# Grouped adaLN modulations and held Strassen quadrants in the down projections; square sums of key and query heads moved behind the next head's products

## The chip, the cores and the metric

One core of a Trainium2 chip runs the whole program. The metric is device time in microseconds of one execution, the median of several. Engines are named as in the profile: PE (matmul) and PEld (its weight loads), DVE, ACT, POOL, and SP, whose queue (SPq) issues nearly all DMAs of the part that is changed.

## The reference

One step of a two-layer encoder on 1152 tokens (1024 of a prompt, 8 x 16 of samples), model width 1024, feed-forward width 2816, all in float32. Layer 0 is RWKV-7 time mixing and a SwiGLU, layer 1 band attention and a SwiGLU. What matters here:

```
mod = silu(c) @ w_ada[l] + b_ada[l]            # 9 rows of c: one prompt, 8 samples; 6*1024 columns per layer
sh_m, sc_m, gt_m, sh_f, sc_f, gt_f = split(mod, 6)
shift, scale = split(silu(c) @ kv_ada_w + kv_ada_b, 2)
h = rmsnorm(x) * (1 + scale) + shift
k = rms_norm(per head of 64: h @ w_k);  v = h @ w_v;  q = rms_norm(per head: hq @ wb_q)
x = x + gt_f * ((silu(h @ w_gate) * (h @ w_up)) @ w_down)      # once in each layer
```

## The kernel before

Activations lie feature by feature: 128 features on the partitions, tokens along the row. Every large float32 product is made of three matmuls (`mm3`): both operands are split into a rounded part (`hi`, an ACT copy, L276) and a rest (`lo`, a DVE subtraction, L277), and hi*hi, hi*lo and lo*hi are summed in PSUM. Tokens are in two groups, `c` = 0 (512) and `c` = 1 (640). The Tile framework's scheduler orders each engine's instructions by a simulated timeline and sets the waits; each engine then runs its own row in order. A tile pool hands out a fixed number of buffers per tag; a new tile waits until a buffer of its tag is released.

The dense part (`dense`) runs after layer 0's time mixing: gate and up products (`gate_up`), the down projection (`down`) of layer 0, then `kv` (keys, values, the first two query heads), attention, and gate, up and down of layer 1.

`down` is one level of Strassen in Winograd's form: seven products `i` in the order 0, 1, 2, 4, 5, 6, 3, each a turn over four blocks `m` of 128 output features. A turn loads its operand from DRAM (`operand`, L1491: `h<-bd`, three pieces for each group, each with a raw, a hi and a lo tile of the tag `h0` or `h1`, 14 buffers each), and each `m` loads 11 weight blocks (`weights`, L1502: `rq<-in_wd` or `rq<-ws`) and issues 33 matmuls of 256 columns (c = 0) and 33 of 320 (c = 1). So both layers' down projections have 7*4*66 = 1848 matmuls. The four output quadrants are summed in `acc`, which `feats` allocates for the whole stage: four buffers of `h0` and four of `h1`. Finished quadrants are added to the residual `x` (`result`, L1529 to L1533; tile `xin` of the 11 buffers of the tag `e`), and in layer 0 their squares are summed (`sqa`).

In layer 0, `down` also computes the modulations of layer 1 and of the keys (`ada_steps`, units 12 to 27). A unit is 512 columns of the weight; four loads of 2 x 256 KB (`aw<-in_wada`, L264), after each of which four matmuls take 32 columns of `scT` (silu(c)) as weights and write the four 32-partition strips of one PSUM bank (`acc<-aw,scT`), the strip standing for a quarter of the contraction; an ACT copy of 512 columns (L226); and four matmuls with the constant `qs` (`acc<-cst,aw`), which sum the strips. `self.step(3)` advances this by three of 64 pieces per block `m`.

In `kv`, `head` computes 128 features of keys or queries of one group, in two parts for c = 1. Each part's `head_norm` copies the product out (ACT), squares it (ACT, L1648), sums the squares by a matmul with the block-ones constant (`acc<-ht,cst` or `O<-ht,cst`), takes the inverse root (`rsqrt2`) and multiplies. Meanwhile `end`, the generator `done`, computes the squares' sum of the next group over all features (`S<-sqa,cst`, `PT<-sqa,cst`) and then its normed features (`normed_split`, L1683 to L1689), which the products need.

Of the kernel before, what the change touches and what calls it, by code (L numbers as in the profile page):

```python
# [76 lines left out]
def prep(i):  # L77
    i = {k: np.asarray(v) for k, v in i.items()}
    d = {}
# [16 lines left out]
    d["wada"] = np.ascontiguousarray(wa.reshape(2, 4, 128, 28, 2, 256).transpose(3, 4, 0, 2, 1, 5)).reshape(28, 4, 128, 1024)  # L96
    par = {f"mix{m}": i["rw_mix"][0, m] for m in range(6)}
# [48 lines left out]
class Trunk:  # L146
# [54 lines left out]
    def ada_steps(self, units, tag="aux", bufs=1, tile=None, sbt=None):  # L201

        nc = self.nc

        def load(u, i):
            w = (tile or self.rawtile)()
            if not isinstance(w, tuple):
                w = w[:, :1024],
            n = 1024 // len(w)
            for j, t in enumerate(w):  # L210
                self.wload(t, self.a["wada"][u, i][:, j * n:(j + 1) * n])
            return [t[:, o:o + 256] for t in w for o in range(0, n, 256)]
        todo = [(u, i) for u in units for i in range(4)]
        ahead = None
        for u in units:
            ps = self.bank(tag, bufs)
            for i in range(4):
                w = ahead or load(*todo.pop(0))
                ahead = load(*todo.pop(0)) if todo and self.fetch_ahead else None
                c = slice(i // 2 * 256, i // 2 * 256 + 256)  # L220
                for q in range(4):
                    mm(nc, ps[32 * q:32 * q + 32, c], self.scT[:, i % 2 * 4 + q, :], w[q], i % 2 == 0, i % 2 == 1)
                if i < 3:
                    yield
# [8 lines left out]
            yield  # L233

# [1157 lines left out]
    def ffn(self, l, B, W, part1, xsrc, dst, done):  # L1392

        nc = self.nc
        spill = self.down_open(l)
        self.gate_up(spill(0), B, iter(W), (0,))
        for _ in part1:
            pass
        self.gate_up(spill(0), B, iter(W), (1,))
        for f in range(1, 22):  # L1400
            self.gate_up(spill(f), B, self.strassen_weights(l, f, nc.vector if f == 1 else None), (0, 1))
            for g in range(32 * (f - 1) // 21, 32 * f // 21):
                self.down_sums(l, g)
        return self.down(l, xsrc, dst, done)
# [61 lines left out]
    def down(self, l, xsrc, dst, done):  # L1466

        nc = self.nc
        gate = 48 * l + 40
# [4 lines left out]
        if l:  # L1474
            turns += [(i, (0, 1)) for i in (6, 3)]
            self.ada = iter(())
        else:
            turns += [(i, (c,)) for c in (1, 0) for i in (6, 3)]
            part512 = lambda: self.ev("aw")[:, 0:512]
            self.ada = self.ada_steps(range(12, 28), "acc", 1, lambda: (part512(), part512()), part512)  # L1480
# [15 lines left out]
        def weights(i, m):  # L1496
            src = {0: 0, 1: 1, 3: 3}.get(i)
            src = self.Ws[m][:, {5: 0, 2: 1, 6: 2, 4: 3}[i]] if src is None else self.a[f"wd{l}"][:, src, m * 1408:(m + 1) * 1408]
# [23 lines left out]
        def result(h, t, m, cs):  # L1522
            f = 4 * h + m
            x = self.ev("xin")[:, 0:576]
            for c in cs:
# [6 lines left out]
                if l == 0:  # L1532
                    squares(c, t, f, o)  # L1533
# [3 lines left out]

        for i, cs in turns:
# [4 lines left out]
            for m in range(4):  # L1543
                W = weights(i, m)
                d = self.wide()[:, 256:832]
                for c in cs:
                    for n, (j, k) in enumerate(ks):
                        s = slice(k * 128, (k + 1) * 128)
                        hi, lo = (X[c][j][h][:, k] for h in range(2))
                        self.mm3(d[:, part[c]], W[j][0][:, s], W[j][1][:, s], hi, lo, n == 0, n == 10)  # L1550
                for c in cs:
# [18 lines left out]
                self.step(3)  # L1570
                for _ in range(2):
                    next(end, None)
            if l == 0 and i == 3:
# [4 lines left out]
        return end  # L1578

    def dense(self, x2, x3, close):  # L1580
# [4 lines left out]
        with ExitStack() as ctx:  # L1585
            pool = lambda n, **k: ctx.enter_context(self.tc.tile_pool(name=n, bufs=1, reuse_waits="tile", **k))
            self.hps = {0: pool("h0")}
            with ExitStack() as c2:
# [13 lines left out]
                def done(c, x, st):  # L1602
                    if c == 1:
                        self.Ak = self.gain("kvn", 104)
                    X[c] = x, self.sq_done(st)
# [35 lines left out]
    def head_norm(self, pz, w, g, out, tag):  # L1641

        nc = self.nc
        nc.scalar.activation(out, pz, AF.Copy)
        aux = self.bank(tag, 1)[:, :w]
        ht = lambda: self.ev("ht", 5)[:, :w]
        v = ht()
        nc.scalar.activation(v, out, AF.Square)  # L1648
        mm(nc, aux, self.C("bo"), v, True, True)
# [4 lines left out]
    def head(self, n, c, W, H, g, dst):  # L1654

        for o, m in ((0, 320), (320, 320)) if c else ((0, 512),):
# [35 lines left out]
    def kv(self, H, X, end):  # L1692
# [5 lines left out]
        nw = 3  # L1698
        W = [self.halves(self.a["wk"][n]) for n in range(nw)]
# [7 lines left out]
        for n in range(nw, 8):  # L1707
            W = self.halves(self.a["wk"][n])
            for c in (1, 0):
# [3 lines left out]
        for n in range(4):  # L1713
            W = [h for u in range(2) for h in self.halves(self.a["wv"][n, u])]
            for c in range(2):
                for w in range((4, 5)[c]):
                    ws = slice(w * 128, (w + 1) * 128)
                    pz = self.wide()[:, 0:256]
                    for k in range(8):
                        ks = slice(k % 2 * 256, (k % 2 + 1) * 256)  # L1720
                        wh, wl = W[k // 2]
                        self.mm3(pz, H[c][0][k][:, ws], H[c][1][k][:, ws], wh[:, ks], wl[:, ks], k == 0, k == 7)
                    vt = self.ev("vt")[:, 0:256]
# [9 lines left out]
        for n in range(2):  # L1733
# [5 lines left out]
            if n == 0:  # L1739
                for e in range(2):  # L1740
                    self.qprep(0, e)
# [370 lines left out]
```

## Time and profile before

| | us |
|---|---|
| median of 3 runs (lowest, highest) | 3791.01 (3785.09, 3791.89) |
| the profiled execution | 3785.41 |
| its span, first to last instruction | 3783.6 |
| busy: PE, PEld, DVE, ACT, POOL | 3457.2, 3088.6, 2248.3, 1667.9, 769.7 |
| first product of down, layer 0 | 1807.26 |
| first key product | 2132.34 |
| first value product | 2275.43 |
| first product of down, layer 1 | 3518.13 |

The profiled execution's time lies 1.8 us above its span, and 5.6 us below the median of the three runs. The table's last four rows are starts in the timeline of PE. A stage that PE fills is read from the rows of PE: how long a run of matmuls takes and what stands between the runs. A timeline row merges like instructions: start, time from the first start to the last end, engine, line, operation, out<-in, shape, count, and in brackets the idle time ahead and who ended it. Float32 matmuls that are not split are recorded twice each (four matmuls of `aw` give x8).

### The profile page before, as it was taken

How to read it: one execution, taken by the hardware profiler on the slowest of the kernel's cores; microseconds unless marked ns; L12 is line 12 of the kernel's file. 1: busy time of each engine (PE TensorE's matmuls, PEld its weight loads, DVE VectorE, ACT ScalarE, POOL GpSimd, SP SyncE). 2: the span in 40 equal slices, each digit the busy share in tenths (PEclk: the TensorE clock that was granted, in tenths of full speed). 3: DMA queues.
4: the chain of work that ended last, by engine and by line, in shares of the span. 5: the costliest groups of instructions: out<-in, count | busy, mean ns of one | idle time of the engine just before them, and what ended most of it. 6: DMA issues, size and time to landing. Idle time of an engine off the chain costs nothing.

```text
span 3783.6 us, 74619 instructions
## 1 busy us (share of the span) xinstructions
PE 3457.2 (91%) x29078; PEld 3088.6 (82%) x29078; DVE 2248.3 (59%) x4380; ACT 1667.9 (44%) x3182; POOL 769.7 (20%) x743
## 2 busy tenths in 40 slices
PE   5788989999889799999999899789888899999999
PEld 3677768777667699999888879677667799999999
DVE  4666666765446765555446742666575776555555
ACT  4545546554223533333344452556564433333342
POOL 0000000000011066676100000000000156667100
PEclk9887899889689899999999999899999899999999
DMA  5776676677666434445788322445565334444764
GB/s 209 233 220 166 199 217 190 194 202 211 180 186 201 141 127 142 139 138 160 265 319 294 123 73 93 144 143 160 159 205 172 133 123 148 143 139 142 243 205 138
DMA packets 548579, 664.12 MB, mean 176 GB/s; under 512 B 137056, under 2 KB 409440, under 8 KB 543744
## 3 DMA queue, kind: packets, MB, share of 16 engines
q1 hardware_dynamic: 472912, 560.62, 46.7%
q0 software_dynamic: 22224, 80.36, 7.0%
q10 hardware_dynamic: 53088, 18.36, 2.1%
q8 instruction: 229, 3.75, 0.4%
q14 instruction: 126, 1.03, 0.1%
HBM read 482.63 MB, written 176.53 MB: 174 GB/s over the span
## 4 chain that ended last, share of the span: by engine, by line
PE 65%; DMA 13%; DVE 10%; issue 6%; ACT 4%; SPq 1%; POOL 1%; ACTq 0%; DVEq 0%; POOLq 0%
PE S L143 30%; PE PT L143 14%; PE acc L143 12%; PE st L143 3%; PE O L143 2%; DMA raw<-in_rw_o 1%; DVE h L277 1%; PE G L143 1%; PE PT L1937 1%; PE aux L143 1%; DMA TT<-Z 1%; DVE wlo L277 1%; DMA bt<-in_rel 1%; DMA xin<-x 1%; DMA h<-bd 1%
## 5 line engine op out<-in xcount | busy, mean ns | idle before, releaser
L143 PE MATMUL S<-h,w 128*128 128x256 f32 (+1 forms) x7374 | 1036.6, 299 | 23.9 <-ACT h L276 7.4
L143 PEld LDWEIGHTS S<-h,w 128*128 128x128 f32 x7374 | 1002.4, 191 | 46.2 <-issue 19.1
L276 ACT ACTIVATE w<-rq 128x512 fp32r<-128x512 f32 (+1 forms) x500 | 304.4, 614 | 661.4 <-PE S L143 290.0
L277 DVE TENSOR_TENSOR w<-rq,w 128x512 fp32r<-128x512 f32 (+1 forms) x500 | 384.4, 773 | 286.6 <-ACT w L276 247.9
L143 PE MATMUL PT<-h,w 128*128 128x256 f32 (+1 forms) x3714 | 532.0, 298 | 10.2 <-DVE h L277 3.8
L143 PE MATMUL acc<-mx,whi 128*128 128x384 f32 x1728 | 505.9, 370 | 37.2 <-ACT whi L276 15.4
L143 PEld LDWEIGHTS PT<-h,w 128*128 128x128 f32 x3714 | 506.4, 190 | 20.5 <-issue 7.8
L143 PEld LDWEIGHTS acc<-mx,whi 128*128 128x128 f32 x1728 | 335.5, 203 | 67.9 <-ACT whi L276 20.1
L143 PE MATMUL acc<-mx,wlo 128*128 128x384 f32 x864 | 314.9, 365 | 9.0 <-DVE wlo L277 9.0
L1373 POOL TENSOR_TENSOR t<-t,t 128x576 f32<-128x576 f32 (+1 forms) x132 | 221.9, 1682 | 262.9 <-ACT t L1380 154.0
L277 DVE TENSOR_TENSOR h<-h,h 128x1024 fp32r<-128x1024 f32 (+6 forms) x152 | 169.3, 1125 | 121.2 <-ACT h L276 111.2
L276 ACT ACTIVATE h<-h 128x1024 fp32r<-128x1024 f32 (+6 forms) x152 | 142.8, 950 | 147.8 <-DMA h<-bd 110.0
L143 PEld LDWEIGHTS acc<-mx,wlo 128*128 128x128 f32 x864 | 174.1, 202 | 21.6 <-DVE wlo L277 13.9
L277 DVE TENSOR_TENSOR wlo<-raw,whi 128x1024 fp32r<-128x1024 f32 x114 | 139.0, 1221 | 83.6 <-ACT whi L276 82.7
L276 ACT ACTIVATE whi<-raw 128x1024 fp32r<-128x1024 f32 x114 | 119.6, 1053 | 128.7 <-PE acc L143 61.6
L143 PE MATMUL S<-h,wh 128*128 128x320 f32 (+1 forms) x744 | 148.5, 348 | 12.7 <-DVE h L1685 4.7
L143 PE MATMUL acc<-h,wh 128*128 128x256 f32 (+1 forms) x864 | 137.9, 309 | 18.4 <-ACT wh L276 9.1
L1373 DVE TENSOR_TENSOR t<-S,t 128x576 f32<-128x576 f32 (+1 forms) x117 | 86.6, 740 | 113.9 <-PE S L143 113.9
L143 PEld LDWEIGHTS S<-h,wh 128*128 128x128 f32 x744 | 123.4, 195 | 31.3 <-ACT wh L276 6.3
L143 PEld LDWEIGHTS acc<-h,wh 128*128 128x128 f32 x864 | 121.2, 200 | 27.2 <-ACT wh L276 9.8
L1303 POOL TENSOR_TENSOR h<-h,h 128x256 f32<-128x256 f32 x12 | 11.0, 942 | 569.9 <-DMA vf<-in_wo 569.9
L1767 POOL MEMSET qbd<- 128x128 f32 x1 | 0.2, 204 | 560.8 <-PE S L143 560.8
(455 smaller groups left out, 5625.8 us busy)
## 6 DMA issues: line engine op xcount, KB each, us to landing
aw<-in_wada SPq DMA_DIRECT2D x128, 256.0 KB, 5.3
bd<-t SPq DMA_DIRECT2D x154, 160.0 KB, 1.9
rq<-in_wg SPq DMA_DIRECT2D x88, 256.0 KB, 2.9
rq<-in_wu SPq DMA_DIRECT2D x88, 256.0 KB, 2.6
ws<-in_wd SPq DMA_DIRECT2D x64, 352.0 KB, 3.6
ws<-ws SPq DMA_DIRECT2D x64, 352.0 KB, 3.3
bd<-t SPq DMA_DIRECT2D x152, 128.0 KB, 1.8
rq<-ws SPq DMA_DIRECT2D x72, 256.0 KB, 3.4
```

The costliest lines, as they stand in the source:

```text
L143: return nc.tensor.matmul(out, lhsT, rhs, start=start, stop=stop)
L276: self.nc.scalar.activation(hi, x, AF.Copy)
L277: self.nc.vector.tensor_tensor(lo, x, hi, ALU.subtract)
L1303: gp.tensor_tensor(out[j], x[j], y[j], op)
L1373: return eng.tensor_tensor(out, x, y, ALU.add)
L1767: nc.gpsimd.memset(self.qbd, 0.0)
L1937: nc.tensor.transpose(pt[:, j * 128:(j + 1) * 128], P[:, j * 128:(j + 1) * 128], self.C("ident"))
```

## The change

Modulations in layer 0's `down`: `ada_groups` replaces `ada_steps` for those 16 units. A unit is now 1024 columns, and a strip stands for 256 output columns instead of a quarter of the contraction, so a unit is 8 loads deep. Two depths are one step: 8 matmuls, the first of which holds the others behind it (`issue_after`), in 32 steps. The same 128 loads of 256 KB are made from a rearranged weight (`wadb`); of a step's two depths the first is loaded into two `e` buffers, the second into the two buffers of the tag `ws`, which the sums of down weights used before (`spare`). Eight copies of 256 columns and 8 x 2 closing matmuls (`acc<-aw,aw`, with the constant `qg`) take the place of 16 copies of 512 and 16 x 4 matmuls. A step is taken after every 44 matmuls of the projection.

On PE, the first modulations of layer 0's down projection; `S` is the PSUM tile of a block `m`, `h` operand pieces, `w` weights, and a row `x2` is two matmuls. Before:

```order
L143 MATMUL S_20087<-h_19934,w_20078 128x320
L143 MATMUL acc_20040<-aw_20041,scT 32x256 x2
L143 MATMUL S_20087<-h_19934,w_20077 128x320
L143 MATMUL S_20087<-h_19935,w_20077 128x320
L143 MATMUL S_20087<-h_19934,w_20078 128x320
L143 MATMUL acc_20040<-aw_20042,scT 32x256 x2
L143 MATMUL S_20087<-h_19934,w_20077 128x320
```

And now:

```order
L145 MATMUL S_20204<-h_19911,w_20188 128x256
L145 MATMUL acc_20027<-ws_20024,scT 32x256 x2
L145 MATMUL acc_20027<-ws_20023,scT 32x256 x2
L145 MATMUL acc_20027<-aw_20020,scT 32x256 x2
L145 MATMUL acc_20027<-aw_20019,scT 32x256 x2
L145 MATMUL S_20204<-h_19910,w_20189 128x256
```

The pairs that stood apart between the projection's matmuls now stand in one run of eight. Over the whole stage, PE's row had 54 runs of modulation matmuls (of 1, 2, 3, 4, 6 and 8 such rows: 29, 10, 1, 5, 8 and 1 times) and 16 runs of strip sums; it now has 35 (29 of four rows, 6 of two) and 8.

Down projection of layer 1: `down_last` replaces `down`. Its sums are three held tiles per group (`T[0]`, `T[2]`, `T[4]`), allocated with their turns, so that one to three `h0` and `h1` buffers are held where four were; finished quadrants go to a tile `o` of the tag `e`, both groups in one row, and are added to the residual in one instruction of 576 columns (or 448 and the samples' 128).

On SP's queue, right behind the last stores of layer 1's gate and up results (`bd<-t`). Before:

```order
L1418 DMA bd_1_3_2_32902<-t_38649 128x320
L1502 DMA rq_39108<-in_wd 128x512
L1502 DMA rq_39114<-in_wd 128x512
L1502 DMA rq_39120<-in_wd 128x384
L1529 DMA xin_39195<-x_110 128x256
...
L1502 DMA rq_39302<-in_wd 128x512
L1491 DMA h_39072<-bd_0_1_0_32873 128x1024
L1491 DMA h_39090<-bd_1_1_0_32894 128x1280
```

And now:

```order
L1475 DMA bd_1_3_2_32852<-t_38599 128x320
L1648 DMA h_39016<-bd_0_1_0_32823 128x1024
L1648 DMA h_39034<-bd_1_1_0_32844 128x1280
L1659 DMA rq_39052<-in_wd 128x512
L1659 DMA rq_39058<-in_wd 128x512
L1659 DMA rq_39064<-in_wd 128x384
L1648 DMA h_39022<-bd_0_1_1_32824 128x1024
```

The operand loads of turn 1 (`h<-bd`, second index 1) stood behind 30 rows, 22 loads of `xin` and eight of weights; they now start in the next row, and those of turn 2 start 13 rows after them.

Keys and queries: `head_norm` is cut in two at the square. The second half, from the square sum's matmul on, is emitted four of eight contraction steps into the next head's products (`head_end`). `kv` computes head 3 of group 1 first, so four heads of group 1 stand ahead of group 0's; head 3's weights are loaded and split once more for group 0. `done` yields once more before its square sum.

On PE, the end of key head 6 and the begin of head 7 (`S_24605` and then `S_24665` is head 6 of group 0, 512 columns; the next `S` and `PT` are head 7 of group 1). Before:

```order
L143 MATMUL S_24665<-h_23878,wh_24584 128x512
L143 MATMUL O_24653<-ht_24654,cst 128x320
L143 MATMUL acc_24692<-ht_24693,cst 128x512
L143 MATMUL S_24716<-h_23218,wh_24706 128x320
L143 MATMUL PT_24755<-h_23218,wh_24706 128x320
```

And now:

```order
L145 MATMUL S_24605<-h_23782,wh_24524 128x512
L145 MATMUL O_24618<-ht_24603,cst 128x320
L145 MATMUL acc_24669<-ht_24642,cst 128x512
L145 MATMUL S_24656<-h_23217,wh_24646 128x320
L145 MATMUL PT_24695<-h_23217,wh_24646 128x320
```

The scheduler has put the square sums where they stood. Among the first heads they do move: those of group 1 now stand 12 to 21 matmuls into the next part, and group 0's sum over all features (`PT<-sqa,cst`) stands behind two parts of products where it stood behind nearly four:

```order
L145 MATMUL S_23731<-h_23220,wh_23699 128x320
L145 MATMUL acc_23744<-ht_23729,cst 128x320
L145 MATMUL PT_23770<-sqa_20559,cst 128x512
L145 MATMUL S_23827<-h_23217,wh_23793 128x320
```

This last piece is of the changed kernel; `S_23731` is the second part of head 3.

The diff, cut to its core:

```diff
+    def ada_groups(self, spare):
...
+        ev = lambda: self.ev("aw")[:, 0:512]
+        steps = [(u, k) for u in range(8) for k in range(8)]
+        def load(n):
+            W = []
+            for (u, k), new in zip(steps[n:n + 2], (ev, spare)):
+                t = [new() for _ in range(2)]
+                for h in range(2):
+                    nc.sync.dma_start(t[h], self.a["wadb"][u, k][:, 512 * h:512 * h + 512])
+                W.append([x[:, o:o + 256] for x in t for o in (0, 256)])
+            return W
+        def close(u, sb):
+            ps = self.bank("acc", 1)
+            for j in range(2):
+                mm(nc, ps[:, j * 36:(j + 1) * 36], sb[:, j * 128:(j + 1) * 128], qg, True, True)
...
+        for n in range(0, 64, 2):
...
+            todo = [(k + j, q, W[j][q]) for j in (1, 0) for q in (3, 2, 1, 0)]
+            lead = product(*todo.pop(0))
+            with self.tc.issue_after(lead.ins):
+                for x in todo:
+                    product(*x)
...
+            if n < 62:
+                W = load(n + 2)
+            yield
...
-            part512 = lambda: self.ev("aw")[:, 0:512]
-            self.ada = self.ada_steps(range(12, 28), "acc", 1, lambda: (part512(), part512()), part512)
+        spare = lambda: self.wq.tile([128, 4, 176], F32, tag="ws", ..., bufs=2).rearrange("p a b -> p (a b)")[:, 0:512]
+        self.ada = self.ada_groups(spare)
...
+                        count += 3
+                        if count >= 44:
+                            count -= 44
+                            self.step()
...
-                self.step(3)
...
+    def down_last(self, gate, xsrc, dst):
...
+        def hold(n):
+            T[n] = [self.slot(c)[:, :4 * (256, 320)[c]].rearrange("p (m t) -> p m t", m=4) for c in range(2)]
...
+        for i in (0, 1, 2, 4, 5, 6, 3):
+            X = operand(i)
+            if i in (0, 2, 4):
+                hold(i)
...
     def head(self, n, c, W, H, g, dst):
...
-            x = self.halfraw()[:, :m]
-            self.head_norm(pz, m, g, x, self.one())
-            self.nc.sync.dma_start(dst[:, n, 512 * c + o:512 * c + o + m], x)
+                if k == 3:
+                    self.head_end()
+            self.ending = self.head_tail(pz, n, m, g, dst[:, n, 512 * c + o:512 * c + o + m])
+            next(self.ending)
...
     def kv(self, H, X, end):
         nw = 3
+        self.head(nw, 1, self.halves(self.a["wk"][nw]), H, kn[:, 0:1], self.kT)
+        for _ in range(3):
+            next(end, None)
         W = [self.halves(self.a["wk"][n]) for n in range(nw)]
...
-            for c in (1, 0):
+            for c in (1, 0)[n == nw:]:
                 self.head(n, c, W, H, kn[:, 0:1], self.kT)
...
-            if n == 0:
-                for e in range(2):
-                    self.qprep(0, e)
+                if n and not c:
+                    for e in range(2):
+                        self.qprep(0, e)
+        self.head_end()
```

More of the change, by code (lines that the diff above doesn't have):

```diff
@@ L233, in ada_steps, with product @@
             yield
+    def ada_groups(self, spare):
+        nc = self.nc
+        qg = self.ev("aw")[:, 0:36]
+        nc.sync.dma_start(qg, self.a["qg"])
+        ev = lambda: self.ev("aw")[:, 0:512]
[12 more added lines that the diff above has]
+                mm(nc, ps[:, j * 36:(j + 1) * 36], sb[:, j * 128:(j + 1) * 128], qg, True, True)
+            o = 48 + u * 8
+            bo = PAR["bada"] + o
+            view = lambda t: t.rearrange("p (g j) n -> p g j n", j=2)
+            bv = view(self.par[:, bo:bo + 8].rearrange("p (f o) -> p f o", o=1).broadcast_to([128, 8, 9]))
+            for j in range(2):
+                pv = ps[:, j * 36:(j + 1) * 36].rearrange("p (g n) -> p g n", n=9)
+                nc.vector.tensor_tensor(view(self.mod[:, o:o + 8, :])[:, :, j], pv, bv[:, :, j], ALU.add)
+        W, last = load(0), None
+        for n in range(0, 64, 2):
+            if last:
+                close(*last)
+                last = None
+            if steps[n][1] == 0:
+                ps = self.bank("acc", 1)
+            u, k = steps[n]
+            todo = [(k + j, q, W[j][q]) for j in (1, 0) for q in (3, 2, 1, 0)]
+            def product(at, q, w):
+                return mm(nc, ps[32 * q:32 * q + 32, 0:256], self.scT[:, at, :], w, at == 1, at == 6)
+            lead = product(*todo.pop(0))
+            with self.tc.issue_after(lead.ins):
+                for x in todo:
+                    product(*x)
+            if k == 6:
+                last = u, ev()[:, 0:256]
+                nc.scalar.activation(last[1], ps[:, 0:256], AF.Copy)
+            if n < 62:
+                W = load(n + 2)
+            yield
+        close(*last)
     def gain(self, name, sc):
@@ L1403, in ffn @@
                 self.down_sums(l, g)
-        return self.down(l, xsrc, dst, done)
+        if l:
+            return self.down_last(48 * l + 40, xsrc, dst)
+        return self.down(48 * l + 40, xsrc, dst, done)
     def down_open(self, l):
@@ L1464, in down_sums, with down @@
         nc.sync.dma_start(self.Ws[m][:, :, j * 176:(j + 1) * 176], q)
-    def down(self, l, xsrc, dst, done):
+    def down(self, gate, xsrc, dst, done):
         nc = self.nc
-        gate = 48 * l + 40
         ks = [(j, k) for j, n in enumerate((4, 4, 3)) for k in range(n)]
@@ L1473, in down @@
         turns = [(i, (0, 1)) for i in (0, 1, 2, 4, 5)]
[L1474 to L1478, printed above, removed]
-            part512 = lambda: self.ev("aw")[:, 0:512]
-            self.ada = self.ada_steps(range(12, 28), "acc", 1, lambda: (part512(), part512()), part512)
+        turns += [(i, (c,)) for c in (1, 0) for i in (6, 3)]
+        spare = lambda: self.wq.tile([128, 4, 176], F32, tag="ws", name=self.nm("ws"), bufs=2).rearrange("p a b -> p (a b)")[:, 0:512]
+        self.ada = self.ada_groups(spare)
         acc, end = {}, iter(())
@@ L1531, in result @@
                 nc.sync.dma_start(dst[:, f, at], o)
-                if l == 0:
-                    squares(c, t, f, o)
+                squares(c, t, f, o)
         def add(o, a, b):
             nc.vector.tensor_tensor(o, a, b, ALU.add)
+        count = 0
         for i, cs in turns:
@@ L1569, in down @@
                     result(*{1: (0, 0), 5: (0, 1), 6: (1, 1), 3: (1, 0)}[i], m, cs)
-                self.step(3)
                 for _ in range(2):
                     next(end, None)
-            if l == 0 and i == 3:
+            if i == 3:
                 for g in (self.ada, end):
@@ L1604, in done @@
                         self.Ak = self.gain("kvn", 104)
+                    yield
                     X[c] = x, self.sq_done(st)
@@ L1641, in head_norm, with head_norm_steps @@
     def head_norm(self, pz, w, g, out, tag):
+        for _ in self.head_norm_steps(pz, w, g, out, tag):
+            pass
+    def head_norm_steps(self, pz, w, g, out, tag):
         nc = self.nc
         nc.scalar.activation(out, pz, AF.Copy)
-        aux = self.bank(tag, 1)[:, :w]
         ht = lambda: self.ev("ht", 5)[:, :w]
@@ L1648, in head_norm @@
         nc.scalar.activation(v, out, AF.Square)
+        yield
+        aux = self.bank(tag, 1)[:, :w]
         mm(nc, aux, self.C("bo"), v, True, True)
@@ L1661, in head, with head_end, head_tail @@
                 self.mm3(pz, wh[:, s], wl[:, s], H[c][0][k][:, o:o + m], H[c][1][k][:, o:o + m], k == 0, k == 7)
-            x = self.halfraw()[:, :m]
-            self.head_norm(pz, m, g, x, self.one())
-            self.nc.sync.dma_start(dst[:, n, 512 * c + o:512 * c + o + m], x)
+                if k == 3:
+                    self.head_end()
+            self.ending = self.head_tail(pz, n, m, g, dst[:, n, 512 * c + o:512 * c + o + m])
+            next(self.ending)
+    ending = iter(())
+    def head_end(self):
+        for _ in self.ending:
+            pass
+    def head_tail(self, pz, n, m, g, dst):
+        x = self.halfraw()[:, :m]
+        yield from self.head_norm_steps(pz, m, g, x, self.one())
+        self.nc.sync.dma_start(dst, x)
     def head_steps(self, n, c, o, m, W, H, g, dst):
```

73 lines of the change are left out of this document (72 added, 1 removed).

## The prediction

> **What bounds the kernel now.** I read the page's busy line and chain first, then busy time by stage, then PE's timeline in the stages that the change touches, then who was waited for there.
>
> ```profile
> PE 3457.2 (91%) x29078; PEld 3088.6 (82%) x29078; DVE 2248.3 (59%) x4380; ACT 1667.9 (44%) x3182; POOL 769.7 (20%) x743
> PE 65%; DMA 13%; DVE 10%; issue 6%; ACT 4%; SPq 1%; POOL 1%; ACTq 0%; DVEq 0%; POOLq 0%
> ```
>
> PE fills 91% of the span and carries 65% of the chain. In its stages only two things give time back: matmuls taken off its row, and waits in it. By stage (window, length, busy time of PE, PEld, DVE, ACT, POOL, granted clock, DMA share, GB/s):
>
> ```profile
> 1890.00:1950.00 60.00, 58.83 (x489) 50.82 (x488) 27.19 (x43) 24.67 (x38) 0.00 (x0) 1.00 0.93 337
> 1920.00:1940.00 20.00, 20.00 (x163) 18.07 (x159) 6.90 (x11) 10.71 (x17) 0.00 (x0) 1.00 1.02 385
> 2132.30:2275.40 143.10, 126.21 (x628) 104.51 (x626) 73.25 (x143) 74.50 (x157) 0.00 (x0) 0.96 0.18 60
> 3558.00:3572.00 14.00, 13.22 (x84) 12.93 (x85) 8.96 (x9) 7.45 (x12) 0.00 (x0) 0.77 0.53 193
> 3600.00:3616.00 16.00, 12.70 (x80) 12.08 (x81) 7.98 (x10) 5.89 (x7) 0.00 (x0) 0.89 0.68 214
> 3616.00:3779.00 163.00, 162.88 (x1218) 162.62 (x1216) 88.94 (x160) 56.88 (x90) 0.00 (x0) 1.00 0.52 166
> ```
>
> Layer 0's down projection (first two rows) is PE-bound with the DMA engines near full. The keys (third) have 16.9 us without PE. Layer 1's down projection (last three) runs full only from 3616 on; before that PE waits, and its clock falls to 0.77 and 0.89.
>
> The yardstick is that full stretch, from the chain in order of time, and the ends of both projections from PE's timeline:
>
> ```profile
> 3629.40 8.79 PE PT L143 x66
> 3638.19 17.59 PE S L143 x132
> ...
> 1807.26 3.18 PE L143 MATMUL PT<-h,w 128*128 128x256 f32 x25
> 2132.34 2.07 PE L143 MATMUL S<-h,wh 128*128 128x320 f32 x13
> 3518.13 3.27 PE L143 MATMUL S<-h,w 128*128 128x256 f32 x26
> 3773.76 5.12 PE L143 MATMUL S<-h,w 128*128 128x256 f32 x34
> ```
>
> 198 matmuls take 26.38 us, 0.1332 each, so the 1848 of one projection need 246.2. Layer 0's takes 2132.34 - 1807.26 = 325.1: 78.9 too many. Layer 1's takes 3778.9 - 3518.1 = 260.8: 14.6 too many. These two surpluses are nearly all that the change can reach.
>
> **Modulations in layer 0.** What a run of them costs is the distance to the next matmul of the projection:
>
> ```profile
> 1825.48 0.62 PE L143 MATMUL acc<-aw,scT 128*32 128x256 f32 x4 [1.46 <-DMA aw<-in_wada]
> 1826.03 0.71 PE L143 MATMUL S<-h,w 128*128 128x320 f32 x3
> ...
> 1974.76 0.64 PE L143 MATMUL acc<-aw,scT 128*32 128x256 f32 x8
> 1975.33 3.74 PE L143 MATMUL S<-h,w 128*128 128x256 f32 x29
> 1978.91 0.96 PE L143 MATMUL acc<-cst,aw 128*128 128x16 f32 x8
> 1979.72 3.36 PE L143 MATMUL S<-h,w 128*128 128x256 f32 x22
> 1983.01 1.07 PE L143 MATMUL acc<-aw,scT 128*32 128x256 f32 x16
> 1984.01 2.46 PE L143 MATMUL S<-h,w 128*128 128x320 f32 x15
> ```
>
> Two matmuls cost 0.55 us, four 0.57, eight 1.00: four strips run together, and a torn run wastes half. With the order's counts, the old 54 runs cost about 41 us (29 x 0.55, 10 x 0.57, 5 x 1.00; the ten longer ones at 0.45 for each four, 14 in all), the 16 strip sums 16 x 0.81 = 13.0. PE's idle time in the stage is 7.5 us, and the sum of squares takes 1.8. Of the 78.9, 15 are left, which I put down to re-entering the projection: 15 / 70 runs = 0.21 each. The trace doesn't show that mechanism apart; its bounds are 0 and 0.21.
>
> New: 29 x 1.00 + 6 x 0.57 = 32.4. The closing matmuls, 36 columns wide, don't occur in the trace; each pair lies between 0.2 us (a quarter of a strip sum) and 0.81 (a whole one); I take half, 0.4, as two of four are issued: 8 x 0.4 = 3.2. Re-entry 43 x 0.21 = 9.0. Together 44.6 instead of 69: 24 us less on PE, and with the bounds 18 to 25. The copies on ACT (eight of 256 columns for sixteen of 512) and the constant's small load lie beside PE, which is the fuller engine.
>
> What the change adds is a wait. The loads for a step's second depth have two buffers, so they can only be asked for when PE has read the last pair.
>
> ```profile
> L264 SPq DMA_DIRECT2D aw<-in_wada x128: 327/383/1521, 1822.7 to 2071.9; - x128
> DMA to landing us min/median/max: 2.6/5.3/7.9
> ```
>
> The pair is free half-way through a step's run and needed at the next one: 44 x 0.1332 + 0.21 + 0.5 = 6.6 us later. Two issues (0.38 each) and the median landing make 6.1, the quickest 3.4, the slowest 8.7. So at the median nothing waits, at the worst 2.1 us in each of 32 steps, 67 us. Were landings spread evenly over 2.6 to 7.9, the mean wait would be 0.4 us, 13 in all; the long landings before belong to bursts of six or seven loads, and pairs go out mostly alone now, so I take 0.25, 8 us. What waits behind it: every later projection matmul, as PE runs in order, and on SP's queue the weight loads behind the pair's. The first load's wait (1.46) may stay. Net for the stage: -24 + 8 = -16.
>
> The DMA engines carry the same bytes in less time: 337 GB/s at a share of 0.93 would become about 355 (337 x 325 / 309) at 0.98. The Trainium skill (DMA: Bandwidth & Descriptors, Where 436 GB/s comes from) puts the HBM limit for one core at about 358 GB/s, which would leave no room in this stretch of the stage; by it, gains beyond 6% there would be lost, 2 us at most. The row at 1920 moved 385 GB/s, so on this core the limit lies higher, and the sum stays.
>
> **Held quadrants in layer 1.** PE waits for the operands of turns 1 and 2:
>
> ```profile
> 3558.10 0.58 PE L143 MATMUL S<-h,w 128*128 128x256 f32 x1 [3.45 <-ACT h L276]
> 3559.36 2.72 PE L143 MATMUL S<-h,w 128*128 128x256 f32 x11 [0.68 <-DVE h L277]
> ...
> 3607.68 0.39 PE L143 MATMUL PT<-h,w 128*128 128x256 f32 x1 [2.28 <-ACT h L276]
> ...
> 3550.70 0.90 SPq L1491 DMA_DIRECT2D h<-bd  x2
> ```
>
> The load behind the first wait goes out at 3550.70, since the quadrants hold four of 14 buffers and a turn needs nine, and because it stands behind the `xin` loads. With one buffer held, all of turn 1's raw tiles fit beside turn 0's, and the order issues them right behind the stores, some 15 us earlier; the landing was about 6. So waits of 3.45 + 0.68 + 2.28 and some 1.3 of smaller ones go, 7.7 us, and the slow clock that follows them: 14 x 0.23 + 16 x 0.11 = 5.0. That is 12.7 of the 14.6; 0.94 at the start stays. I take -12, between 0 (operands are late for another reason) and -13.7. What could be late next are weights (`rq<-in_wd`), which share SP's queue with the earlier operand loads; at a DMA share of 0.6 there is room.
>
> The Trainium skill (TensorE: Matmul & The Clock Gate, What's actually happening) has the clock halved after an idle window of about 3.4 us, until as long a busy one has passed. By it only the first wait brings a slow spell, about 1.7 us lost, and the gain would be 9 to 10. The trace agrees with the fall after the 3.45 wait (0.77 over 14 us), but shows 0.89 around the 2.28 one as well, so I keep 12.
>
> At the end:
>
> ```profile
> 3778.92 0.82 DVE L1536 TENSOR_TENSOR h<-S,h 128x256 f32<-128x256 f32 x2 [7.12 <-PE S L143]
> 3779.66 0.94 DVE L1174 SCALAR_TENSOR_TENSOR h<-h,mod,xin 128x256 f32<-128x256 f32 x2
> ```
>
> Two additions, then one residual of 576 columns (about 0.8) where the first store went out after one of 256 (0.5): +0.3.
>
> **Keys and queries.** PE's waits from 2132 to 2276:
>
> ```profile
> PE S L143 <- DVE h L1685: 4.7, 2, 3.0
> PE acc L143 <- ACT ht L1648: 4.2, 5, 1.1
> PE O L143 <- ACT ht L1648: 3.6, 3, 1.3
> PE PT L143 <- DVE kk L337: 2.6, 1, 2.6
> ...
> 2143.10 12.77 PE L143 MATMUL S<-h,wh 128*128 128x320 f32 x67 [1.65 <-DVE h L1685]
> 2153.28 0.43 DVE L1520 TENSOR_TENSOR sqa<-sqa,kk 128x256 f32<-128x256 f32 x1 [0.53 <-ACT kk L1519]
> 2156.25 1.02 PE L143 MATMUL PT<-sqa,cst 128*128 128x512 f32 x2
> ```
>
> Square sums waited 4.2 + 3.6 = 7.8. The order leaves those of the later heads where they were, with their waits of about 1.2; among the first heads some three waits of a microsecond go, and most of the 2.6 behind `PT`. Against that, `PT<-sqa,cst` now stands two parts earlier: PE gets there about 7 us before 2156.25, at 2149 to 2150, and the last square is there at 2153.7: a new wait of some 4 us. The extra split of head 3's weights (1.4 us on DVE) may delay the 4.7. Bounds: -8 (all square sums) and +5 (the new wait and nothing gained); I take -1. Value blocks and the two query heads keep their order: 0.
>
> **Sum.** -16 - 12 + 0.3 - 1 = -28.7 on the profiled 3785.41 gives 3756.7; on the median of the runs, 5.6 higher, 3762. I predict 3759.
>
> **Rivals.**
> 1. Just-in-time pairs make it slower. Without them the change gains 24 + 12 + 1 = 37, so it turns at 37 / 32 = 1.16 us per step; the slowest landing gives 2.1, 67 us: 3785 + 30 = 3815. For it: the DMA share of 0.93. Against: the median leaves 0.5 us of slack, and a waiting PE also thins the traffic. Chance 0.05.
> 2. The pairs and the crowded DMA engines take two thirds of layer 0's gain: -24 + 18, in all -19: 3766 to 3772. Chance 0.20.
> 3. Layer 1's operands come earlier, but PE waits for weights instead: -4 in place of -12, in all -21: 3764 to 3770. Chance 0.10.
> 4. Pairs never wait, and the keys' waits go too: -24 - 13 - 7 = -44: 3741 to 3747. Chance 0.15.
> 5. Several terms fail together and nothing beyond 0.2% is left: 3780 to 3790. Chance 0.05.
>
> The forecast has 0.45, with 3750 to 3765 as its own range. 3738 to 3776 takes in rivals 2, 3 and 4 and leaves 1 and 5, and the outer ends of the bounds, outside. Faster by over 0.2% (7.6 us, about what can be told from no change) holds for the forecast and rivals 2 to 4: 0.90; 0.05 each for the rest.
>
> **What will show it.** Layer 0's projection should last about 309 us (325 before), with runs of x16 a microsecond long and the waits for `ws<-in_wadb` summing below 10 us; over 25 means rival 2, over 37 rival 1. Layer 1's should last about 249, at a clock of 1.00 throughout, with no wait for `h` above 1 us. The keys should show one wait of 3 to 5 us at `PT<-sqa,cst` and end-of-head waits as before. If layer 0's runs of eight cost more than 1.1 us, strips don't run together in the new order, and the first term falls.

## The result, and the profile after

The changed kernel takes 3775.6 us (median of 10 runs, 3764.3 to 3788.8) where the kernel before takes 3792.6 in the same series: a ratio of 0.9949, 95% interval 0.9934 to 0.9965. By that ratio it is 19 us (13 to 25) faster; the medians are 17 us apart. A second series (e12 below) gave 0.9947 (0.9925 to 0.9968). One run of e1, one of e3 and one of the kernel before took 11% to 86% longer than the others of their kernel, and the ratios leave them out. The prediction had 3759, with 3750 to 3765 as the forecast's own range and 3738 to 3776 as the outer one. The sign is right, and the gain is about 60% of what was forecast: 3775.6 lies outside the forecast's own range and 0.4 us inside the end of the outer one. The profiled execution, 3766.4 us with a span of 3764.6, is among the quicker ones.

The stages, from PE's timeline of the changed kernel (start, length, engine, line, operation, shape, count): the first row of layer 0's down projection, of the keys, of layer 1's down projection, and the last.

```profile
1801.87 3.15 PE L145 MATMUL PT<-h,w 128*128 128x256 f32 x25
...
2129.42 3.31 PE L145 MATMUL S<-h,wh 128*128 128x320 f32 x20
...
3512.22 3.27 PE L145 MATMUL S<-h,w 128*128 128x256 f32 x26
...
3750.38 8.95 PE L145 MATMUL S<-h,w 128*128 128x256 f32 x66
```

Layer 1's projection ends at 3759.3 and lasts 247.1 us (260.8 before). Layer 0's lasts 327.5, which is longer than the 325.1 before, although its matmul work shrank. The waits of PE in that stage tell where the gain went (who waited for whom: total, times, longest), first of the kernel before:

```profile
PE S L143 <- DVE sqa L1520: 3.5, 1, 3.5
PE acc L143 <- DMA aw<-in_wada: 1.6, 2, 1.5
```

and of the changed kernel:

```profile
PE S L145 <- DVE sqa L1572: 10.9, 1, 10.9
PE acc L145 <- DMA ws<-in_wadb: 5.2, 2, 3.7
PE PT L145 <- DVE h L1587: 3.2, 2, 2.2
PE S L145 <- ACT h L331: 3.2, 3, 1.7
PE S L145 <- DVE h L332: 2.0, 3, 0.8
```

With the smaller ones PE waits 26 us where it waited 7.3. The runs of modulations themselves came out as costed:

```profile
1965.40 0.64 PE L145 MATMUL acc<-ws,scT 128*32 128x256 f32 x8
1965.85 0.61 PE L145 MATMUL acc<-aw,scT 128*32 128x256 f32 x8
1966.40 4.41 PE L145 MATMUL S<-h,w 128*128 128x320 f32 x32
...
1981.22 0.53 PE L145 MATMUL acc<-aw,aw 128*128 128x36 f32 x4
1981.58 4.46 PE L145 MATMUL PT<-h,w 128*128 128x256 f32 x32
```

Eight matmuls (two rows of x8) take 1.00 us, a closing pair 0.36. And each of the two long waits is followed by a slow clock (window, length, busy PE, PEld, DVE, ACT, POOL, granted clock, DMA share, GB/s):

```profile
1824.60:1827.00 2.40, 2.35 (x18) 1.08 (x19) 0.00 (x0) 0.00 (x0) 0.00 (x0) 0.50 1.01 382
1827.00:1837.00 10.00, 10.00 (x64) 10.00 (x64) 1.95 (x3) 1.79 (x3) 0.00 (x0) 0.81 0.61 210
...
2102.50:2107.00 4.50, 4.47 (x15) 3.69 (x16) 0.91 (x2) 2.23 (x4) 0.00 (x0) 0.50 0.35 110
```

That is 0.5 x 2.4 + 0.19 x 10 = 3.1 us lost behind the first and 0.5 x 4.5 = 2.2 behind the second.

The wait of 10.9 us has a history, which the chain of work in order of time shows. In the kernel before, a loop through DVE, SP's queue and the DMA engines was already on the chain at that place:

```profile
2084.17 0.21 DVE h L1179
2084.38 0.02 issue
2084.40 0.32 SPq L1531
2084.72 0.05 issue
2084.76 0.02 SPq L1529
2084.78 0.03 issue
2084.81 4.39 DMA xin<-x
```

DVE finishes a residual, SP issues its store (`x<-h`), right behind it the load of the next `xin`, and DVE waits for that landing. In the changed kernel the same loop runs straight into PE's square sum (`S<-sqa,cst`, here the head of the last row):

```profile
2090.25 4.02 DMA xin<-x
2094.30 0.56 DVE h L1229
2095.29 2.29 DMA xin<-x
2097.61 0.56 DVE h L1229
2098.56 2.31 DMA xin<-x
2100.89 0.56 DVE h L1229
2101.48 0.48 ACT kk L1571
2101.98 0.50 DVE sqa L1572
2102.53 13.04 PE S L145 x83
```

One turn of the loop costs 3.3 us with a landing of 2.3, and 5 to 9 us between 2067 and 2086, where DVE starts these residuals at 2066.9, 2075.8, 2080.7 and 2085.8. PE finished group 1's last product at about 2076.6 (before: 2093.0); the square sum could start at 2102.5 (before: 2105.0). In PE's timeline, first of the kernel before:

```profile
2104.96 2.50 PE L143 MATMUL S<-sqa,cst 128*128 128x320 f32 x4 [3.48 <-DVE sqa L1520]
...
2102.53 2.50 PE L145 MATMUL S<-sqa,cst 128*128 128x320 f32 x4 [10.92 <-DVE sqa L1572]
```

Of the 16 us that PE came earlier by the clock of the trace (5.4 of them from ahead of this stage), the loop passed on 2.5. Counted from the stage's first product, the square sum starts 300.7 us in, where it started 297.7 us in: the work that PE was spared did not bring the end of the loop forward.

### The profile page after: what moved, and what is told of

Its sections match the earlier page's. It is cut to its first block, busy times and chain, and to the rows that moved or that the text cites. A ratio compares the mean times of both kernels' runs of the same rounds, so it can differ in the third digit from the quotient of the medians.

```text
span 3764.6 us, 74365 instructions
## 1 busy us (share of the span) xinstructions
PE 3433.4 (91%) x28982; PEld 3079.2 (82%) x28982; DVE 2244.8 (60%) x4366; ACT 1660.5 (44%) x3176; POOL 769.9 (20%) x743
## 4 chain that ended last, share of the span: by engine, by line
PE 65%; DMA 13%; DVE 10%; issue 6%; ACT 4%; SPq 1%; POOL 1%; ACTq 0%; DVEq 0%; POOLq 0%
PE S L145 30%; PE PT L145 14%; PE acc L145 12%; PE st L145 3%; PE O L145 2%; PE PT L2098 1%; DMA raw<-in_rw_o 1%; DVE h L332 1%; PE aux L145 1%; PE G L145 1%; DMA TT<-Z 1%; PE Y L145 1%; DMA h<-bd 1%; DVE wlo L332 1%; DMA Z<-T 1%
## 5 line engine op out<-in xcount | busy, mean ns | idle before, releaser
L145 PE MATMUL PT<-h,w 128*128 128x256 f32 (+1 forms) x3714 | 527.2, 297 | 10.3 <-DVE rq L1428 3.8
```

Source lines behind the costliest of these rows:

```text
L145: return nc.tensor.matmul(out, lhsT, rhs, start=start, stop=stop)
```

## The experiments

Totals scatter by up to 25 us among runs of one kernel, so the stages were compared as well, each read from PE's timeline of one profiled execution. The columns are lengths in us: layer 0's down projection; keys; values to the end of layer 1's gate and up products; layer 1's down projection; and all of them. The last column is the ratio to the kernel before, by the timed runs.

| kernel | down 0 | keys | between | down 1 | sum | ratio (95%) |
|---|---|---|---|---|---|---|
| before | 325.1 | 143.1 | 1242.7 | 260.8 | 1971.6 | |
| changed | 327.5 | 138.0 | 1244.8 | 247.1 | 1957.5 | 0.9949 (0.9934 to 0.9965) |
| e12, changed again | 326.1 | 140.0 | 1242.3 | 246.4 | 1954.8 | 0.9947 (0.9925 to 0.9968) |
| e1, modulations only | 326.2 | 139.2 | 1239.7 | 258.3 | 1963.3 | 0.9963 (0.9951 to 0.9975) |
| e2, held quadrants only | 326.4 | 144.4 | 1246.9 | 247.2 | 1964.8 | 0.9975 (0.9958 to 0.9992) |
| e3, keys and queries only | 332.9 | 136.8 | 1242.0 | 257.2 | 1968.8 | 0.9969 (0.9955 to 0.9984) |
| e4, stores on POOL's queue | 321.2 | 134.3 | 1248.9 | 246.5 | 1950.9 | 0.9924 (0.9898 to 0.9949) |
| e6, xin asked for early | 322.6 | 139.2 | 1241.6 | 246.4 | 1949.8 | 0.9938 (0.9914 to 0.9962) |
| e8, pairs in e | 327.4 | 137.5 | 1241.0 | 247.1 | 1952.9 | 0.9932 (0.9911 to 0.9952) |
| e11, xin in ws | 307.5 | 136.3 | 1240.6 | 247.4 | 1931.8 | 0.9906 (0.9874 to 0.9937) |
| e5, xin in ws and early | 308.4 | 136.4 | 1237.4 | 246.9 | 1929.1 | 0.9889 (0.9868 to 0.9909) |
| e7, e5 and POOL's queue | 307.8 | 136.7 | 1247.3 | 247.5 | 1939.3 | 0.9898 (0.9878 to 0.9918) |
| e9, before with xin in ws, early | 325.8 | 134.6 | 1245.2 | 259.5 | 1965.1 | 0.9976 (0.9959 to 0.9994) |
| e10, e5 with the old heads | 310.6 | 136.9 | 1241.0 | 247.3 | 1935.8 | 0.9900 (0.9876 to 0.9924) |

**The parts alone.** e1 is the kernel before with `ada_groups` in place of `ada_steps`:

```diff
-            self.ada = self.ada_steps(range(12, 28), "acc", 1, lambda: (part512(), part512()), part512)
+            self.ada = self.ada_groups(spare)
```

> The kernel before with only the grouped modulations in layer 0's down projection. The changed kernel's trace has that stage at 1801.87 to 2129.42, 327.5 us against 325.1, although its runs of eight cost 1.00 us as forecast. Theory A (the end of the stage is held by the chain of residual loads, residuals and stores behind the sum of squares, which has not moved): PE saves 10 to 16 us and waits that much longer for sqa, so the wait ahead of S<-sqa,cst is 12 to 18 us (3.5 before), the stage lasts 322 to 328 and the kernel takes between -4 and +3 us against before. Rival B (the two-buffer pairs are what eats the gain): the waits for ws<-in_wadb sum to over 10 us and the wait for sqa stays below 6. Rival C (the fourth head and the added yield spoil layer 0's end, not the groups): with neither of them here the stage is 305 to 312 long and the kernel 12 us or more faster.

```profile
PE S L145 <- DVE sqa L1575: 9.5, 1, 9.5
PE acc L145 <- DMA ws<-in_wadb: 3.9, 2, 2.9
```

The stage (326.2) and the place of the wait are theory A's; rival C falls, and so does B: the pairs' waits stay small. The wait is shorter than A's 12 to 18, but others beside it grew: 23 us in all in this stage, against 7.3. The kernel is faster by 14 us (10 to 19), more than A had. Of the profiled execution's stages, the first two account for 2.8 of these, the others for 5.5, and the rest shows in none (see the last section). The three parts alone (e1, e2, e3) were timed at 14, 9.5 and 12 us, 35 together, where the whole change is worth 19; by the sums of the stages they are worth 8.3, 6.8 and 2.8, 18 together, where the whole is worth 14.

e2 has `down_last` for layer 1 alone:

```diff
+        if l:
+            return self.down_last(48 * l + 40, xsrc, dst)
         return self.down(l, xsrc, dst, done)
```

> The kernel before with only the held quadrants of layer 1's down projection. In the changed kernel's trace that stage lasts 247.1 us (3512.22 to 3759.33) against 260.8. If this part works alone: 247 to 249 us with no wait for h over 1 us, the clock at 1.00, and the kernel 12 to 14 us faster, which is two thirds of the whole change (19 us). If it needs the other parts: under 8 us.

The stage lasts 247.2: the whole gain of 13.6 us is there without the other parts. The timed ratio gives 9.5 us, less than the 12 to 14 expected, with an interval (3 to 16) that holds them.

e3 has the heads cut in two, the fourth head ahead and the extra `yield`:

```diff
                 def done(c, x, st):
...
+                    yield
                     X[c] = x, self.sq_done(st)
...
+        self.head(nw, 1, self.halves(self.a["wk"][nw]), H, kn[:, 0:1], self.kT)
+        for _ in range(3):
+            next(end, None)
```

> The kernel before with only the change of keys, queries and the extra yield ahead of the sum of squares. In the changed kernel's trace the keys last 138.0 us against 143.1, and from the values to layer 1's down projection 1244.8 against 1242.7. If the parts add up: keys 137 to 140, the kernel 2 to 6 us faster. If the 5 us of the keys come only from arriving late (operands already there, since PE had waited 10.9 us for sqa just before): keys 141 to 144 and the kernel within 2 us of before.

The keys get 6.3 us shorter and the stage ahead of them 7.8 longer: together 469.7 against 468.2, so nothing is gained up to the first value product. In the longer stage PE waits 10.3 us (7.3 before), 2.3 of them at an addition of DVE just ahead of the keys, and the granted clock is 0.93 in the first 50 us and 0.84 in the last 33 (1.00 and 0.94 in the first 50 and the last 25 before). Neither expectation foresaw that; the timed ratio (12 us faster, 6 to 17) is not explained by any stage that the edit touches.

**The chain of residual loads.** e4 takes the stores off SP's queue:

```diff
-                nc.sync.dma_start(dst[:, f, at], o)
+                nc.gpsimd.dma_start(dst[:, f, at], o)
```

> The changed kernel with the stores of layer 0's finished quadrants (x<-h) on POOL's queue instead of SP's, so that no load of xin stands behind a store that waits for a residual. Theory A1 (SP's order makes the chain load, residual, store, load, of 3.3 us for each result): the residuals of group 1 come up to a landing earlier each, the wait for sqa falls from 10.9 to below 4 us, the kernel is 6 to 10 us faster than the changed one. Rival A2 (the xin load waits for the buffer that the last residual frees, whatever stands ahead on SP): the residuals stay 3.3 us apart, the wait stays at 9 to 12, same time within 2 us. Rival A3 (the DMA engines, near full up to 2060, deliver late): the landings of xin stay at 4 to 6 us up to there, and the wait falls by 3 us at most.

```profile
2108.84 2.50 PE L145 MATMUL S<-sqa,cst 128*128 128x320 f32 x4 [5.06 <-DVE sqa L1572]
```

The wait halves and the stage is 6 us shorter: between A1 and A3. DVE still waited for a landing at most residuals, and the last six of group 1 started 3.1, 3.3, 3.8, 1.5 and 3.0 us apart, nearly the spacing that A2 had. So the store's place in SP's queue was only a part of the loop.

e6 asks for `xin` at the beginning of its block of products, from the same buffers `e`; e8 leaves `xin` alone and loads both depths of a modulation step into `e`:

```diff
+                xs = fetch(*RES[i], m, cs) if i in RES else None      # e6, behind weights(i, m)
...
-        spare = lambda: self.wq.tile([128, 4, 176], F32, tag="ws", ...
+        spare = lambda: self.ev("aw")[:, 0:512]                       # e8
```

> The changed kernel with the loads of xin asked for at the beginning of their block, still from the buffers e: a control for the run with xin in its own two buffers. In the order the loads still stand right behind the stores of the last result. Theory A1 (what counts is that a load stands behind the store of the residual before it): as the changed kernel, wait for sqa 9 to 12 us, time within 3 us. Rival (asking early is enough): wait below 5, 6 us or more faster.

> The changed kernel with both depths of a modulation step loaded into the buffers e, none into the two of the tag ws; nothing else changed. If the just-in-time pairs cost what the prediction took (0.25 us for each of 32 steps): waits of the modulations fall from 5.4 us to under 2, and the stage gets 3 to 5 us shorter at most, less what then waits for sqa. If they cost nothing beyond the first load's wait: the stage lasts 325 to 330 as now, with the time taken from the modulations added to the wait for sqa. If the buffers e were short: waits for xin grow and the kernel is 3 us or more slower.

e6 brings 5 us in the stage and leaves a wait of 8.3: mostly A1, a little of the rival. e8 settles the pairs. Without them the modulations wait no less:

```profile
PE acc L145 <- DMA aw<-in_wadb: 9.9, 6, 4.3
PE PT L145 <- DVE h L1587: 6.8, 2, 4.6
```

The modulations wait 9.9 us instead of 5.4, and the stage stays at 327.4, as its second expectation had it, but that one had the wait for `sqa` grow, and here none is left. The second row is the same chain in another place: DVE runs its row in order, so an addition that frees a PSUM bank stands behind a residual that waits for `xin`, and PE waits for the bank ahead of the square sum (the residual starts at 2103.64, the addition at 2104.58, PE at 2105.14).

e11 differs from e8 by one line (beside the definition of `two`), which gives `xin` the two `ws` buffers; e5 has the early request as well:

```diff
         def result(h, t, m, cs):
             f = 4 * h + m
-            x = self.ev("xin")[:, 0:576]
+            x = two()          # two buffers of the tag ws
```

> The changed kernel with the two ws buffers given to xin instead of the modulations (which take all four tiles of a step from the buffers e), and each load of xin asked for at the beginning of its block of products, so that a load can stand one result ahead. With stores moved to POOL's queue the residuals came closer but the wait for sqa was still 5.1 us. Theory A (the chain of residual loads holds the end of layer 0's stage): with loads a result ahead the residuals of group 1 follow PE's results, the wait for sqa falls below 4 us, and from the first product of that stage to the end the kernel takes 5 to 10 us less than the changed one (1957.5). Rival B (the pairs were the delay): the two waits for ws<-in_wadb (5.2 us) go as well. Rival C (layer 0's DMA engines are full up to 2060, and lateness there is passed on in whatever order): the wait stays at 8 to 12 us, no gain.

> The changed kernel with xin in the two ws buffers (and the modulations' four tiles in the buffers e), but each load of xin asked for where it was, behind its block's products. With both edits the stage of layer 0's down projection lasted 308.4 us and the wait for sqa was gone; with the early request alone 322.6 and 8.3 us. In the order the load now stands one store earlier without being asked for early. If the own buffers are what counts (the eleven e buffers, shared with the modulations, held each load back until the last residual): stage 307 to 312, no wait for sqa above 1 us, 20 us or more below the changed kernel. If the early request is needed as well: stage 316 to 324, wait 4 us or more.

On SP's queue the order of the loads and stores of group 1's results in turn 6 (rows of weights and operands left out) is, in the changed kernel,

```
DMA xin_22578<-x_108 128x320
DMA x_109<-h_19951 128x320
DMA xin_22657<-x_108 128x320
DMA x_109<-h_19951 128x320
DMA xin_22730<-x_108 128x320
```

and e11

```
DMA ws_22578<-x_108 128x320
DMA ws_22657<-x_108 128x320
DMA x_109<-h_19951 128x320
DMA ws_22730<-x_108 128x320
DMA x_109<-h_19951 128x320
```

where the two stores of the result ahead are left out. A load now stands one store ahead, and the loop is open. In e11's trace DVE waits for a landing once among these residuals, 0.8 us, and the square sum starts without a wait, in the middle of a run of products:

```profile
2074.83 0.55 DVE L1229 SCALAR_TENSOR_TENSOR h<-h,mod,ws 128x320 f32<-128x320 f32 x1 [0.80 <-DMA ws<-x]
2077.77 0.55 DVE L1229 SCALAR_TENSOR_TENSOR h<-h,mod,ws 128x320 f32<-128x320 f32 x1
```

```profile
2080.00 1.96 PE L145 MATMUL PT<-h,w 128*128 128x256 f32 x15
2081.80 1.24 PE L145 MATMUL S<-sqa,cst 128*128 128x320 f32 x4
2082.64 2.56 PE L145 MATMUL PT<-h,w 128*128 128x256 f32 x18
```

The last residual of group 1 starts at 2077.77, 275.7 us into the stage; in the changed kernel it starts at 2100.89, 299.0 us in. The scheduler orders all rows anew after each edit, and it has put the square sum further forward as well: 48 products behind group 1's last one, where it was 79 in the changed kernel. PE finds it ready even there.

The stage lasts 307.5 (e11) and 308.4 us (e5). One line is worth 20 us of this stage, the early request nothing more. By the medians of the runs of one series, e5 lies 17.6 us below e8, and e11 17.8 below the changed kernel (e12), a little less than the 20 that e11's expectation asked for. Theory A of e5 had the place right, but only 5 to 10 us for it: from the stage's first product on, e5 takes 28 us less than the changed kernel. Rival C of e5, that the load on the DMA engines holds the stage, falls, as its B does (the modulations still wait 6.0 us). e5 has the lowest ratio of the study, 42 us (35 to 50) below the kernel before, where the changed one is 19 below; the intervals of e7, e10 and e11 overlap with its own.

e7 adds POOL's stores to e5.

> Both remedies: xin in its own two buffers and asked for early, and the stores on POOL's queue. Theory A: the wait for sqa falls below 3 us, and the time from the first product of layer 0's down projection to the end is 8 to 14 us below the changed kernel's 1957.5; the whole is the fastest version. If the DMA engines or the operands of the second half are the limit: no better than the stores alone (1950.9).

No wait for `sqa` is left to remove, and the stage stays at 307.8. Its sum is 18 us below the changed kernel's, more than the 8 to 14 expected, but e5 without POOL's stores is 28 below; e7 gains nothing on e5 (its sum is 10 us longer, all of it between the keys and layer 1's down projection, which the edit doesn't touch).

e9 gives the kernel before the own buffers and the early request:

> The kernel before with only the remedy: in layer 0's down projection xin is loaded into the two ws buffers, asked for at the beginning of its block. The modulations are the old ones. In the kernel before, PE waited 3.5 us for sqa and 0.2 for the square ahead of it, and the stage lasted 325.1 us. Theory A (the chain of residual loads was there before, hidden behind PE by all but 3.7 us): the wait for sqa goes, the stage lasts 319 to 323, the kernel is 3 to 8 us faster than before, so the remedy is worth 28 us behind the grouped modulations (1929.0 against 1957.5 from the stage's first product) and a quarter of that ahead of them. Rival (the remedy helps in another way, whichever modulations are used): 15 us or more faster.

```profile
2110.99 1.24 PE L143 MATMUL S<-sqa,cst 128*128 128x320 f32 x4
...
2136.60 5.60 PE L143 MATMUL PT<-h,w 128*128 128x256 f32 x33 [2.43 <-ACT wh L276]
```

The wait for `sqa` goes as expected, but the stage doesn't get shorter (319 to 323 was expected): other waits take its place (6.8 us in all against 7.3), among them the second row's, and the gain appears in the keys (stage and keys together 460.4 against 468.2). The kernel is 9 us faster (2 to 16). The rival falls: from the first product on, the remedy is worth 6.5 us here (1965.1 against 1971.6) and 24 behind the grouped modulations (1929.1 in e5 against 1952.9 in e8, which differ by the remedy alone).

e10 is e5 with the old heads:

> The kernel with xin in its own two buffers (stage 308.4 us, keys 136.4), with the whole change of keys and queries undone: heads as before, no fourth head ahead, no extra yield. If the head change is worth what the keys of the changed kernel show (138.0 against 143.1): keys 140 to 144, layer 0's stage plus keys 448 to 452 instead of 444.8, the kernel 3 to 7 us slower than that one. If the keys only profited from arriving later at operands that were ready: layer 0's stage plus keys within 2 us of 444.8.

Stage and keys take 447.5 against 444.8: the head change is worth 2.7 us at most, between the two expectations, and no more than the stages scatter (e12). The keys last 136.9 with old heads as well, and 139.2 in e1, so most of the 5 us by which the changed kernel's keys are shorter does not come from the heads.

e12 is the changed kernel once more.

> The changed kernel once more, on the same chip as the run beside it: how far its stages repeat. Expected: layer 0's down projection 325 to 330 us with a wait for sqa of 9 to 12, keys 136 to 140, layer 1's down projection 246 to 248, and everything ahead of the dense part anywhere from 1294 to 1313 us, since no edit of this study touches it and it came out at 1294.9 to 1312.1 so far.

```profile
2106.97 2.50 PE L145 MATMUL S<-sqa,cst 128*128 128x320 f32 x4 [10.24 <-DVE sqa L1572]
```

All stages repeat within 2.5 us. The stretch between the keys and layer 1's projection differs by more, 1239.7 to 1246.9, among the kernel before, e1, e2 and e9, whose code there is the same.

## Why the prediction was right or wrong

**Modulations, PE's work (-24): right, and hidden.** In e5 the stage without its 13 us of waits is 295.2 long; before, without 7.3, it was 317.8. That is 22.6 less. In the changed kernel itself the work shows once the waits are taken off: 327.5 without 26.2 of waits and 5.3 of slow clock is 296.0. The stage of 309 that the prediction gave is what e5 and e11 reach (308.4, 307.5), and not what the change itself reaches.

**The pairs (+8): too high, and for a wrong reason.** The modulations waited 5.4 us (1.6 before), and 3.7 of them at the first step; the 31 steps behind it waited 1.7, where 0.25 each was said. With other buffers the modulations wait 9.9 (e8) and 6.0 (e5): the two buffers of the tag `ws` are not the cause, and rivals 1 and 2, which rest on them, don't describe what happened, though the total came out near rival 2's.

**The missing term: the step that failed is the net for this stage, which costed everything outside PE and the pairs at nothing.** The 3.5 us wait ahead of `S<-sqa,cst` was in front of me, inside the "7.5 us of idle time", and I treated it as a constant. It was the visible end of a loop whose own pace set its end, and a PE that comes earlier only waits longer at it: 10.9 us here, plus the slower clock behind it, and in e8 4.6 at a PSUM bank in its place. The prediction asked what its own new loads would hold up, but not what hid the loads of `xin`, nor what they cost when that cover is gone. The rows were to be had: the chain in order of time, read inside the stage and not only at its end, named `DMA xin<-x` there.

**Held quadrants (-12): right.** 13.6 in the changed kernel, 13.6 alone. The waits for `h` went but for one, and the clock is full throughout:

```profile
PE S L145 <- DVE h L332: 0.5, 1, 0.5
```

```profile
3512.20:3536.00 23.80, 23.31 (x178) 23.11 (x177) 15.75 (x17) 6.77 (x12) 10.21 (x9) 1.00 0.69 233
3536.00:3600.00 64.00, 64.00 (x480) 64.00 (x480) 34.24 (x47) 28.42 (x44) 0.00 (x0) 1.00 0.72 242
3600.00:3759.00 159.00, 159.00 (x1195) 159.00 (x1194) 86.26 (x146) 54.98 (x87) 0.00 (x0) 1.00 0.56 180
```

PE's waits in the stage fell from 8.5 us to 0.5. The other 5.6 of the gain are about the 5.0 that the prediction took for the slow clock around both waits, so it had to be counted. The Trainium skill (TensorE: Matmul & The Clock Gate, What's actually happening) would have given 9 to 10, with a slow spell for the longest wait alone. For layer 0 of the changed kernel it fits: 0.50 right behind the waits of 3.7 and 10.9 us. In layer 1 before, the trace goes against it: behind the wait of 2.28 us the granted clock was 0.53 and 0.50 from 3608.7 to 3612.0. Weights were not late, so rival 3 falls. The end grew by 0.6 us where 0.3 was said (the last store's work lies 5.3 us before the span's end instead of 4.7).

**Keys and queries (-1): small, as said, but for other reasons than the parts named.** The new wait of 4 us at `PT<-sqa,cst` didn't come; PE reaches it late, after the waits ahead of it. The keys lost 5.1 us (3.1 in e12), of which e10 leaves at most 2.7 to the heads; where the rest comes from was not shown.

**The sum.** By stages: +2.5 - 5.1 + 2.1 - 13.6 = -14.1 from the first product of layer 0's down projection, +0.6 at the end, and -5.4 from ahead of it, where the change does nothing: 19.0 of span in the profiled execution (rounded), against -28.7. The mis-sized term is layer 0's stage, +2.5 where -16 was said. That the time still came out inside the outer range, by 0.4 us, is luck: that range was widened for rivals 2 to 4, and none of these describes what happened.

## What to carry to other kernels

A wait that is short now can be the end of a chain with a pace of its own: before crediting saved work on the bounding engine, follow what it waits for backwards through the stage (here residual, store, load, landing) and ask when that chain would be done if the engine came ten microseconds earlier. A load that shares an issuing queue with a store, and buffers with other traffic, can end up strictly behind the store of the previous result; here two buffers of its own let it go one step ahead, and were worth about as much as the whole change (18 us by the runs). When two buffers are to be given away, look first for the loads on the slowest loop: here they were worth more there than with the larger loads of the modulations.

## What the runs showed of the hardware that I had not expected

The part ahead of the dense stage, the same in all these kernels, took from 1294.3 to 1312.1 us in 14 profiled executions. That spread exceeds every single term of this change, so a total is no test of a term of 3 us, and e3's and e1's timed gains beyond their stages stay unexplained. Whether they are this spread or an effect of the edit on the earlier part was not separated.

After a wait of 10.9 us the granted clock was 0.50 for the next 4.5 us. After one of 3.7 us it was 0.50 for the next 2.4 us and 0.81 on average over the ten behind them. In this kernel such a wait costs 2 to 3 us more than its own length.
